# Scaling u out of PSUM, folding the row scale into q's decay factors, loading the skip diagonal, and a new order of table work and S5 in a two-layer hybrid trunk

## The chip, the core and the metric

One Trainium2 chip, one core. Times are microseconds of the core for one execution of the whole program; lower is better. The engines are TensorE (PE, with its weight loads PEld), VectorE (DVE), ScalarE (ACT), GpSimd (POOL) and SyncE (SP), which here issues the transfers. Each engine works through its own row of instructions in order and waits for others by semaphores.

## The reference, cut to what matters

Two layers on an input of 512 rows by 1024 features, all in float32. Each has a mixer and an FFN:

```
for i in range(DEPTH):                      # 2
    h = rmsnorm(x, norm_mix[i]);  z = h @ w_in[i]
    u, q, k, v, g, gate_lr = columns of z   # 512, 256, 256, 512, 512, 16
    y = s5(u)                               # 32 groups of 16 channels -> 64 complex states each
    y = gelu(y);  y = y * sigmoid(y @ w_glu + b_glu);  y_s5 = rmsnorm(y)
    y_gla = gla(q, k, v, g, gate_lr)        # 4 heads, chunks of 64 rows
    x = x + concat([y_s5, y_gla]) @ w_out[i]
    x = x + swiglu(rmsnorm(x))
return rmsnorm(x, norm_final)

# s5: s_t = a * s_(t-1) + bbar u_t;  y_t = Re(c s_t) + d_skip * u_t   (a, bbar, c complex)
# gla: log_a = log_sigmoid(gate_lr @ w_gate + b_gate) / 16;  cum = cumsum(log_a) in each chunk
#      q_dec = q / 8 * exp(cum);  k_inv = k * exp(-cum);  k_end = k * exp(last - cum)
```

## The kernel before

Tiles are 128 partitions by 512 rows of the sequence. Each float32 matrix product is made of three: weights and input are split into a high and a low part (whi, wlo; x0h, x0l and so on), and `mm3` adds whi·xh, whi·xl and wlo·xh (L576 to L578). A dense tile has eight blocks of 128 by 128, so 24 matmuls. The weights come as a stream of units of 1024 columns, eight blocks each: `Weights` loads a unit (raw, L142, SP's queue, two buffers), casts it on ScalarE (whi, L163) and takes the difference on VectorE (wlo, L165), three buffers of each. In layer 0's input projection unit 3 holds u(3), units 4 to 7 q and k of the two head pairs, units 8 to 10 three tiles of g, units 11 to 14 v; wlo3 below is the difference of unit 3.

The row scale rstd of the norm isn't applied to the input; the results are multiplied with it instead. It is made after the first two u tiles (`stats`), as rs_mix on ScalarE. With it VectorE makes rsb (L706), the input of the gate matmul gt (L768). u(b), one of four tiles, is copied by ScalarE in 16 pieces of 32 by 128 from PSUM into the layout U that S5 wants (L745), and then scaled there (L738) by rU, rstd laid out alike (L687). The gates run through `gate_a` (matmul, logistic), `gate_c` (cumulative sum by a scan, L783, L784, L786) and `gate_b` (three exponentials E, Ei, Ee for each head pair hp). `q_tile` multiplies q with E and then, in quarters of 64 by 256, with rstd, into two zeroed buffers qz:

```
nc.vector.scalar_tensor_tensor(e, ps, 0.125, e, op0=M, op1=M)          # L807
...
nc.gpsimd.memset(qz[i][r, :, 1 - d], 0.0)                                # L813
nc.vector.tensor_tensor(qz[i][r, :, d], e[..], R["rstd"][..], op=M)      # L814
```

S5 works in chunks of four rows, with the complex states of a block of channels turned by tables cosT and sinT, so that a real scan does the recurrence. For each of four blocks b: `s5_fwd` makes x (L833) from U and the table Wk, turns it with four products on VectorE (L841 to L844) and two sums on GpSimd (ro, L846, L847), and scans eight times (L852); `s5_back` turns back (L866, L867, L872, L873) with sr and sm on GpSimd (L869, L874); `s5_y` makes y from the tables Tz and Vx (L888, L890), and ScalarE takes the gelu in 16 pieces (L899); `y_split` casts the result for the GLU (yg, L583).

The tables themselves depend on the parameters and are made in the kernel: small vectors a1 to a4, fr, fi (`prep_small`, 128 by 32, L304 and neighbours), complex products (`cplx`, eight operations: four of 128 by 256, L407 to L410, and halves), transposes on VectorE (L441) and copies by DMA into Wk (`prep_w`, L446, four a transpose), Vx and Tz (`prep_v`, with the skip diagonal idd in four operations at L498), cosT and sinT (`prep_rot`: angles rf at L538 to L544, cosines on ScalarE, six operations L567 to L572 on GpSimd for each quarter). Layer 1's tables are made during layer 0's FFN. Layer 0's are made beside its input projection: four generators, moved on by calls of bg() between the tiles, `bg0` with the table BG_W saying which.

PE, ACT and SP issue in the order of the program text. DVE does so in the first part of layer 0's mixer (to `region.close()`) and in the FFN; elsewhere a scheduler orders DVE, and POOL throughout, by priorities and due operands.

## Time and profile before

| | before |
|---|---|
| median of 3 executions | 1160.08 us (1159.53 to 1160.54) |
| profiled execution | 1159.86 us, span 1158.1 us |
| TensorE busy | 1110.1 us (96% of the span), 5316 matmuls |
| VectorE busy | 706.2 us (61%) |
| ScalarE busy | 485.6 us (42%) |
| GpSimd busy | 331.9 us (29%) |

The span runs from the first to the last instruction of the profiled execution; its own time is 1.76 us longer. The shares are averages over the whole program: layer 0's mixer takes the first 170 us or so, its FFN and layer 1 follow, and in the two FFNs TensorE works nearly without a gap. What an engine costs in a stretch is read from that stretch.

### The profile page before, as it was taken

How to read it: one execution, taken by the hardware profiler on the slowest of the kernel's cores; microseconds unless marked ns; L12 is line 12 of the kernel's file. 1: busy time of each engine (PE TensorE's matmuls, PEld its weight loads, DVE VectorE, ACT ScalarE, POOL GpSimd, SP SyncE). 2: the span in 40 equal slices, each digit the busy share in tenths (PEclk: the TensorE clock that was granted, in tenths of full speed). 3: DMA queues.
4: the chain of work that ended last, by engine and by line, in shares of the span. 5: the costliest groups of instructions: out<-in, count | busy, mean ns of one | idle time of the engine just before them, and what ended most of it. 6: DMA issues, size and time to landing. Idle time of an engine off the chain costs nothing.

```text
span 1158.1 us, 13973 instructions
## 1 busy us (share of the span) xinstructions
PE 1110.1 (96%) x5316; PEld 913.9 (79%) x5316; DVE 706.2 (61%) x947; ACT 485.6 (42%) x844; POOL 331.9 (29%) x322
## 2 busy tenths in 40 slices
PE   8789779999999999999999799999999999999997
PEld 5568658888888888888887688888888888888886
DVE  7996976866454454564466994686545444444454
ACT  6853458443232232432358653745323222222243
POOL 6899544546000052065030440352000000000003
PEclk9899889999999999999999999999999999999999
DMA  6155111244343523232331212123332333223221
GB/s 211 55 112 126 37 37 37 92 130 116 103 109 100 137 91 101 82 109 91 93 104 41 73 61 85 56 91 94 107 100 85 106 99 102 91 91 109 91 91 73
DMA packets 64099, 107.72 MB, mean 93 GB/s; under 512 B 37408, under 2 KB 38304, under 8 KB 64032
## 3 DMA queue, kind: packets, MB, share of 16 engines
q1 hardware_dynamic: 63888, 106.56, 30.2%
q8 instruction: 42, 0.69, 0.2%
q10 hardware_dynamic: 144, 0.26, 0.1%
q14 instruction: 25, 0.20, 0.1%
HBM read 100.52 MB, written 2.10 MB: 89 GB/s over the span
## 4 chain that ended last, share of the span: by engine, by line
PE 79%; DVE 12%; ACT 3%; issue 2%; POOL 2%; DMA 1%; SPq 1%; DVEq 0%; POOLq 0%; ACTq 0%
PE fg L576 7%; PE fg L577 7%; PE fg L578 7%; PE fu L578 7%; PE fu L576 7%; PE fu L577 7%; PE fo L578 7%; PE fo L576 7%; PE fo L577 7%; DVE ro L852 2%; DVE wlo L165 2%; ACT U L745 1%; DVE qz L814 1%; DMA wrr<-in_wr_dram 1%; DMA raw<-in_wst_dram 1%
## 5 line engine op out<-in xcount | busy, mean ns | idle before, releaser
L165 DVE TENSOR_TENSOR wlo<-raw,whi 128x1024 fp32r<-128x1024 f32 x182 | 242.2, 1333 | 113.2 <-ACT whi L163 112.0
L163 ACT CAST whi<-raw 128x1024 fp32r<-128x1024 f32 x183 | 191.8, 1050 | 280.0 <-PE fo L577 116.9
L602 POOL TENSOR_TENSOR sq_fin<-sq_fin 128x512 f32<-128x512 f32 x5 | 6.5, 1296 | 341.8 <-ACT sq_fin L598 341.8
L1237 DVE TENSOR_TENSOR fu<-fu,rs_ffn 128x512 f32<-128x512 f32 x44 | 30.4, 691 | 116.7 <-PE fu L578 113.9
L1254 DVE TENSOR_TENSOR xall<-xall,fo 128x512 f32<-128x512 f32 x78 | 53.1, 686 | 61.9 <-PE fo L578 61.7
L1234 DVE TENSOR_TENSOR fg<-fg,rs_ffn 128x512 f32<-128x512 f32 x44 | 30.3, 688 | 34.7 <-PE fg L578 30.8
L1236 ACT ACTIVATE fg<-fg 128x512 f32<-128x512 f32 x44 | 27.7, 629 | 42.5 <-DVE fg L1234 42.4
L899 ACT ACTIVATE y<-y 32x128 f32<-32x128 f32 x128 | 34.4, 269 | 20.9 <-PE y L890 17.3
L1238 DVE TENSOR_TENSOR fu<-fg,fu 128x512 f32<-128x512 f32 x44 | 31.3, 711 | 5.7 <-ACT fg L1236 1.3
L745 ACT COPY U<-u 32x128 f32<-32x128 f32 x128 | 32.9, 257 | 1.5
L852 DVE TENSOR_TENSOR_SCAN ro<-sp_mag,ro 128x128 f32<-128x128 f32 x64 | 28.5, 507 | 6.6 <-POOL ro L846 6.6
L1089 POOL TENSOR_TENSOR xall<-xall,wo 128x512 f32<-128x512 f32 x16 | 25.5, 1613 | 24.0 <-DVE wo L1088 24.0
L407 POOL TENSOR_TENSOR pt<-bc,sp_a1r 128x256 f32<-128x256 f32 x2 | 1.7, 852 | 94.0 <-issue 92.0
L568 POOL TENSOR_TENSOR rt<-rg 128x512 f32<-128x512 f32 x8 | 10.2, 1288 | 59.8 <-ACT rg L548 59.7
L602 POOL TENSOR_TENSOR sq_s<-sq_s,sq_s 128x512 f32<-128x512 f32 x6 | 8.1, 1342 | 64.3 <-ACT sq_s L598 64.3
L869 POOL TENSOR_TENSOR sr<-ro,ro 128x508 f32<-128x508 f32 x8 | 14.6, 1826 | 39.3 <-DVE ro L867 39.3
L602 POOL TENSOR_TENSOR sq_x1nmix<-sq_x1nmix 128x512 f32<-128x512 f32 x7 | 9.2, 1315 | 57.3 <-ACT sq_x1nmix L598 57.3
L890 PE MATMUL y<-sr,Vx 128*128 128x128 f32 x64 | 15.0, 322 | 8.0 <-POOL sr L869 7.8
L890 PE MATMUL y<-sm,Vx 128*128 128x128 f32 x64 | 14.8, 318 | 6.2 <-POOL sm L874 6.2
L888 PE MATMUL y<-U,Tz 128*128 128x128 f32 x64 | 14.9, 320 | 5.5 <-DVE ro L842 5.4
L846 POOL TENSOR_TENSOR ro<-ro,ro 128x512 f32<-128x512 f32 x8 | 10.7, 1344 | 30.8 <-DVE ro L843 30.8
L890 PEld LDWEIGHTS y<-sr,Vx 128*128 128x128 f32 x64 | 11.9, 231 | 8.9 <-POOL sr L869 8.9
(1257 smaller groups left out, 3533.0 us busy)
## 6 DMA issues: line engine op xcount, KB each, us to landing
raw<-in_wst_dram SPq DMA_DIRECT2D x183, 512.0 KB, 3.5
Wk<-wt SPq DMA_DIRECT2D x64, 64.0 KB, 3.9
xall<-in_xt_dram SPq DMA_DIRECT2D x3, 512.0 KB, 8.5
out_dram<-fin SPq DMA_DIRECT2D x6, 256.0 KB, 2.2
bc<-in_s5bc_dram SPq DMA_DIRECT2D x4, 256.0 KB, 4.1
raw<-in_wst_dram SPq DMA_DIRECT2D x1, 384.0 KB, 5.8
cst<-in_const_dram SPq DMA_DIRECT2D x1, 384.0 KB, 5.0
xall<-in_xt_dram SPq DMA_DIRECT2D x1, 283.0 KB, 3.0
```

What stands on the lines that cost most here:

```text
L163: self.nc.scalar.copy(hi, raw)
L165: (self.nc.gpsimd if v in POOL_W else self.nc.vector).tensor_tensor(lo, raw, hi.bitcast(F32), op=ALU.subtract)
L576: nc.tensor.matmul(ps, whi, xh, start=start, stop=False)
L577: nc.tensor.matmul(ps, whi, xl, start=False, stop=False)
L578: nc.tensor.matmul(ps, wlo, xh, start=False, stop=stop)
L745: nc.scalar.copy(u[32 * t:32 * t + 32, j].rearrange("p (n c) -> p n c", n=NCH), pv[32 * j:32 * j + 32, :, t, :],)
L852: v.tensor_tensor_scan(dst[:, cs], sp["mag4"][:, c:c + 1].to_broadcast([P, P]), src[:, cs], 0.0, M, A)
L890: nc.tensor.matmul(o, Vx[:, pr, part, 1:].rearrange("p a b c -> p (a b c)"), s_[:, cs], start=False, stop=(part == 1),)
L899: nc.scalar.activation(yv[32 * j:32 * j + 32, :, t, :], ps[32 * t:32 * t + 32, j * P:(j + 1) * P].rearrange("p (n c) -> p n c", n=NCH), AF ...
L1237: nc.vector.tensor_tensor(u, pu, rstd[0], op=M)
L1238: nc.vector.tensor_tensor(u, g, u, op=M)
L1254: nc.vector.tensor_tensor(xT[n], xT[n], ps[n], op=A)
```

## The change

- u is scaled straight out of PSUM: one product of the tile with rstd into us on VectorE, and ScalarE's 16 copies read us instead of PSUM. rU goes. In layer 0 the copies come later: those of u(1) in `u_tile(3)`, of u(2) behind q(0), of u(3) behind k(0).
- E is multiplied with rstd as a whole (`gate_d`), and qz is written from PSUM with E in four operations. The qz buffers are allotted once and zeroed at the start.
- The skip diagonal is laid out on the host and loaded (64 KB a layer); the four operations of L498 go.
- The product with a4 for layer 0's Vx goes from GpSimd to VectorE.
- A table TABLES takes BG_W's place: at each call, a letter for each step of a generator (s small, w Wk, v Vx, r rotations).
- The scans become a function of their own, `s5_scan`; GpSimd's S5 operations get high priority; x(0) stands ahead of v, and the other S5 steps are spread anew over v's eight parts.

```diff
-    NACT = 45
+    NACT = 41
...
+    qz = [[cp.tile([P, 4, 2, 64], F32, name=f"qz{hp}{i}") for i in range(2)] for hp in range(2)]
...
+        idd = act(f"idd{l}")[:, 0:P]
+        nc.sync.dma_start(idd, s5bc[l][:, 4 * 256:])
...
         for n in (1, 2, 3, 4):
-            cplx(e, l, cr, nci, spv(f"a{n}r", l), spv(f"a{n}i", l),
+            cplx(e[n - 1], l, cr, nci, spv(f"a{n}r", l), spv(f"a{n}i", l),
                  halves(Vx[:, :, 0, n]), halves(Vx[:, :, 1, n]), conj=True)
             yield
-        idd = act(f"idd{l}")
-        for b in range(NB):
-            r = slice(32 * b, 32 * b + 32)
-            nc.vector.tensor_tensor(
-                idd[r, 0:P].rearrange("p (a b) -> p a b", a=4),
-                bcast(C("ident")[r, 32 * b:32 * b + 32], [32, 4, 32], 1),
-                bcast(S(l, "dskip")[r, 4 * b:4 * b + 4], [32, 4, 32], 2), op=M,
-            )
-        yield
...
-                unit_rows()
+                for b in range(2):
+                    u_scale(b, ps[b])
                 if l == 0:
                     bg()
-                u_evac(0, ps[0])
+                else:
+                    u_copy(0)
...
             gate_a(0)
             gate_a(1)
-            u_copy(1, ps[1])
+            u_scale(2, ps2)
+            if l == 0:
+                bg()
+            else:
+                u_copy(1)
             gate_c(0)
             gate_c(1)
-            u_scale(1)
-            u_evac(2, ps2)
+            if l == 0:
+                bg()
+                u_copy(0)
+            else:
+                u_copy(2)
...
+        def u_scale(b, ps):
+            t = us[b] = act(f"us{l}{b}")
+            nc.vector.tensor_tensor(t, ps, R["rstd"], op=M)
...
+        def gate_d(hp):
+            e = E[hp][0]
             d = dec[hp] = cp.tile([P, NCH], F32, tag=f"dec{hp}", name=f"dec{l}{hp}")
             nc.vector.tensor_copy(d, e.rearrange("p (n s) -> p n s", n=NCH)[:, :, 63])
-            E[hp] = (e, ei, ee)
+            nc.vector.tensor_tensor(e, e, R["rstd"], op=M)
...
-            nc.vector.scalar_tensor_tensor(e, ps, 0.125, e, op0=M, op1=M)
...
-                    nc.gpsimd.memset(qz[i][r, :, 1 - d], 0.0)
-                    nc.vector.tensor_tensor(
-                        qz[i][r, :, d], e[r, hf].rearrange("p (n t) -> p n t", n=4),
-                        R["rstd"][r, hf].rearrange("p (n t) -> p n t", n=4), op=M,
+                    nc.vector.scalar_tensor_tensor(
+                        qz[hp][i][r, :, d], ps[r, hf].rearrange("p (n t) -> p n t", n=4), 0.125,
+                        e[r, hf].rearrange("p (n t) -> p n t", n=4), op0=M, op1=M,
                     )
...
             q_tile(0)
+            u_copy(2)
             bg()
             k_tile(0)
+            u_copy(3)
             bg()
...
+            s5_fwd(0)
             bg()
+            s5_scan(0)
             region.close()
...
             v_tiles({
-                0: [bg, bg],
-                1: [lambda: s5_fwd(0), bg],
-                2: [lambda: s5_back(0), bg],
-                3: [lambda: s5_fwd(1)],
-                4: [lambda: score(0), lambda: s5_back(1), bg],
-                5: [lambda: s5_y(0), lambda: s5_fwd(2), bg],
-                6: [lambda: s5_y(1), lambda: s5_back(2), lambda: s5_fwd(3)],
-                7: [lambda: score(1), lambda: s5_back(3)],
+                0: [lambda: s5_back(0), bg],
+                1: [lambda: s5(1), bg],
+                2: [lambda: score(0), bg],
+                3: [lambda: s5_back(1), bg],
+                4: [lambda: s5_y(0), lambda: s5(2), bg],
+                5: [lambda: score(1), lambda: s5_back(2), bg],
+                6: [lambda: s5_y(1), lambda: s5(3)],
+                7: [lambda: s5_back(3)],
             })
+            y_split(0)
             s5_y(2)
-            y_split(0)
             y_split(1)
+            g_tile(3)
             y_split(2)
-            g_tile(3)
             s5_y(3)
...
-        BG_W = (1, 0, 2, 1, 1, 1, 1, 1, 1, 1)
+        TABLES = (
+            "s", "sv", "wr", "w", "ww", "wr", "wwr", "wwr", "wwv", "v", "r", "v", "r", "v", "", "v", "v",
+        )
```

How the rows of instructions change is shown at three places. A row has its line, the operation, out and in, and the shape; x4 means four alike. Line numbers differ between the two kernels.

VectorE in layer 0 around rsb, before (sptmp and sp_ names are small table vectors, rf and rk angles of the rotations, rs_mix the row scale):

```order
L544 TENSOR_TENSOR rf_243<-rf_243,rk_244 128x384
L304 TENSOR_TENSOR sptmp<-lam 128x32 x2
L304 TENSOR_TENSOR sptmp<-sptmp 128x32
L165 TENSOR_TENSOR wlo_306<-raw_199,whi_305 128x1024
L352 RECIPROCAL sptmp<-sptmp 128x32
L706 TENSOR_TENSOR rsb_342<-r_333,rs_mix_358 128x512
L687 COPY rU_370<-rs_mix_358 32x128 x4
```

and of the change:

```order
L305 TENSOR_TENSOR sp_a1i<-sptmp 128x32
L305 TENSOR_TENSOR sp_a1r<-sptmp 128x32
L165 TENSOR_TENSOR wlo_291<-raw_207,whi_290 128x1024
L694 TENSOR_TENSOR rsb_327<-r_318,rs_mix_343 128x512
L732 TENSOR_TENSOR us_355<-u_262,rs_mix_343 128x512
L732 TENSOR_TENSOR us_357<-u_263,rs_mix_343 128x512
L344 TENSOR_SCALAR sptmp<-sp_a1r 128x32
```

rsb and the first two us now stand directly behind wlo3; the angles of the rotations and thirteen small operations that stood ahead come later.

SP's queue in layer 0, from the third group of Wk copies on, before (wt is a transposed table, raw a unit of weights):

```order
L446 DMA Wk<-wt_689 32x16x32 x4
L142 DMA raw_769<-in_wst_dram 128x1024
L446 DMA Wk<-wt_738 32x16x32 x4
L142 DMA raw_824<-in_wst_dram 128x1024
L446 DMA Wk<-wt_790 32x16x32 x4
L142 DMA raw_870<-in_wst_dram 128x1024
L446 DMA Wk<-wt_836 32x16x32 x4
L142 DMA raw_910<-in_wst_dram 128x1024
L446 DMA Wk<-wt_883 32x16x32 x4
L142 DMA raw_957<-in_wst_dram 128x1024
L446 DMA Wk<-wt_930 32x16x32 x4
L142 DMA raw_1025<-in_wst_dram 128x1024
```

and of the change:

```order
L450 DMA Wk<-wt_713 32x16x32 x4
L450 DMA Wk<-wt_761 32x16x32 x4
L142 DMA raw_801<-in_wst_dram 128x1024
L450 DMA Wk<-wt_767 32x16x32 x4
L450 DMA Wk<-wt_813 32x16x32 x4
L142 DMA raw_853<-in_wst_dram 128x1024
L450 DMA Wk<-wt_819 32x16x32 x4
L450 DMA Wk<-wt_866 32x16x32 x4
L142 DMA raw_907<-in_wst_dram 128x1024
L142 DMA raw_958<-in_wst_dram 128x1024
```

Copies and loads alternated; now raw_801 (unit 11), raw_853 (12) and raw_907 (13) each stand behind two groups of copies, and the last four groups close up.

TensorE where the g tiles end and v begins, before (kT is a transpose of Ee, v four tiles at once):

```order
L578 MATMUL g_932<-x7h,wlo_827 128x512
L935 MATMUL kT_966<-cst,Ee_593 128x128 x4
L913 MATMUL v_978<-whi_872,x0h 128x512
L914 MATMUL v_978<-wlo_873,x0h 128x512
```

and of the change:

```order
L573 MATMUL g_933<-x7h,wlo_804 128x512
L936 MATMUL kT_967<-cst,Ee_533 128x128 x4
L827 MATMUL x_974<-U_475,Wk 128x128 x4
L827 MATMUL x_975<-U_475,Wk 128x128 x4
L914 MATMUL v_1010<-whi_855,x0h 128x512
```

x(0) stood behind the first two of v's eight parts (24 matmuls) and now stands ahead of them all.

## Rows read from the trace of the kernel before

**Rows 1.** Page, busy tenths of TensorE in 40 equal slices.

```profile
PE   8789779999999999999999799999999999999997
```

**Rows 2.** Waits of TensorE: line waited for: us in total, times, longest.

```profile
PE y L890 <- POOL sr L869: 7.8, 4, 3.3
...
PE gt L768 <- DVE rsb L706: 5.2, 1, 5.2
```

**Rows 3.** Timelines of ScalarE and VectorE at the gates: start, us, engine, line, operation.

```profile
29.81 0.63 ACT L614 ACTIVATE rs_mix<-rs_mix 128x512 f32<-128x512 f32 x1
...
30.74 4.27 ACT L745 COPY U<-u 32x128 f32<-32x128 f32 x16
...
34.66 1.21 DVE L165 TENSOR_TENSOR wlo<-raw,whi 128x1024 fp32r<-128x1024 f32 x1
...
36.06 0.62 DVE L706 TENSOR_TENSOR rsb<-r,rs_mix 128x512 f32<-128x512 f32 x1
```

**Rows 4.** Window: us, busy PE, PEld, DVE, ACT, POOL, TensorE's clock, DMA share, GB/s.

```profile
20.00:62.00 42.00, 32.52 (x134) 22.43 (x133) 41.06 (x82) 37.44 (x88) 32.71 (x35) 0.92 0.16 51
```

**Rows 5.** VectorE's groups, 20 to 160 us: busy us, mean ns | idle before.

```profile
L498 DVE TENSOR_TENSOR idd<-cst,xall 32x128 f32<-32x128 f32 x4 | 3.9, 973 | 0.1
L738 DVE TENSOR_TENSOR U<-U,rU 128x512 f32<-128x512 f32 x4 | 3.7, 955 | 0.0
...
L784 DVE TENSOR_TENSOR_SCAN ab<-cst,mn 128x512 f32<-128x512 f32 x2 | 3.1, 1528 | 0.1
```

**Rows 6.** Line L814 in layer 0: ns min/median/max, first and last start.

```profile
L814 DVE TENSOR_TENSOR qz<-E,rs_mix x8: 416/870/1193, 71.7 to 83.0; 64x256 f32<-64x256 f32 x8
```

**Rows 7.** Timelines of TensorE and VectorE around q(1), with the idle time before.

```profile
62.38 0.79 PE L578 MATMUL q<-x0h,wlo 128*128 128x512 f32 x1 [2.93 <-DVE wlo L165]
...
63.57 0.42 DVE L407 TENSOR_TENSOR pt<-bb,sp_a1r 128x256 f32<-128x256 f32 x1
...
68.06 1.16 DVE L417 TENSOR_TENSOR wk<-pt 64x256 f32<-64x256 f32 x2
```

**Rows 8.** DMA issues, 0 to 130 us: count, KB each, median us to landing.

```profile
raw<-in_wst_dram SPq DMA_DIRECT2D x17, 512.0 KB, 4.1
Wk<-wt SPq DMA_DIRECT2D x32, 64.0 KB, 3.5
xall<-in_xt_dram SPq DMA_DIRECT2D x3, 512.0 KB, 8.5
```

**Rows 9.** Timelines of SP's queue and TensorE at x(0).

```profile
96.01 2.71 SPq L446 DMA_DIRECT2D Wk<-wt  x4
...
101.47 1.13 PE L833 MATMUL x<-U,Wk 128*128 128x128 f32 x8 [1.00 <-DMA Wk<-wt]
```

**Rows 10.** GpSimd's groups, 26 to 160 us, and its timeline at S5(0)'s sum.

```profile
L415 POOL TENSOR_TENSOR Vx<-pt 64x256 f32<-64x256 f32 x8 | 7.0, 875 | 0.5
L569 POOL TENSOR_TENSOR cosT<-cosT,rt 128x512 f32<-128x512 f32 x4 | 6.1, 1540 | 0.0
...
L567 POOL TENSOR_TENSOR cosT<-rk 128x512 f32<-128x512 f32 x4 | 4.4, 1120 | 0.1
...
112.49 1.29 POOL L846 TENSOR_TENSOR ro<-ro,ro 128x512 f32<-128x512 f32 x1
```

**Rows 11.** VectorE's timeline: the first scans and the end of S5 in layer 0.

```profile
113.81 4.54 DVE L852 TENSOR_TENSOR_SCAN ro<-sp_mag,ro 128x128 f32<-128x128 f32 x4 [4.61 <-POOL ro L846]
...
156.25 0.69 DVE L873 TENSOR_TENSOR rp<-ro,cosT 128x512 f32<-128x512 f32 x1
```

**Rows 12.** Timelines of ScalarE and TensorE ahead of the GLU's last quarter.

```profile
164.39 0.63 ACT L1001 ACTIVATE th<-g 128x512 f32<-128x512 f32 x1 [2.81 <-DVE g L992]
...
170.22 0.50 PE L576 MATMUL gl<-yg03h,whi 128*128 128x512 f32 x1 [3.04 <-ACT yg03h L583]
```

**Rows 13.** Layer 1: timelines of VectorE at the gates and TensorE at y(1).

```profile
624.92 1.18 DVE L784 TENSOR_TENSOR_SCAN ab<-cst,mn 128x512 f32<-128x512 f32 x1
...
660.91 0.49 PE L890 MATMUL y<-sr,Vx 128*128 128x128 f32 x2 [3.32 <-POOL sr L869]
```

115 lines of the change are left out of this document (54 added, 61 removed).

## The prediction, made before the changed kernel was run

> **What bounds the kernel now.** I read the page's slices first, then the waits of TensorE, then the timeline of each engine around those waits, from late to early. The slices are 28.95 us each, and TensorE is 90% busy or more in all but seven [rows 1]: the first three, the fifth and sixth (116 to 174 us), one in layer 1 (637 to 666), the last. In the FFN TensorE works without a gap, so what layer 0's mixer wins or loses ahead of it shifts the end by as much. The waits of TensorE name the places [rows 2]: 5.2 us at the gate matmul for rsb on VectorE, 7.8 us at S5's outputs for sr on GpSimd.
>
> At the gates, ScalarE has rstd ready at 29.81 + 0.63 = 30.44, but VectorE starts rsb only at 36.06, behind table operations and the weight difference of 34.66 [rows 3]. This isn't an idle VectorE that looks away: from 20 to 62 us it is busy for 41.06 of 42.00 us [rows 4]. So the order can be bettered there and the amount of work stays the limit.
>
> The second place is S5. VectorE stands idle for 4.61 us until GpSimd's sum ro (started at 112.49, behind rotation tables) lets the first scans start at 113.81 [rows 10, 11]. From there VectorE works nearly without a break through the four blocks of S5, to 156.25 + 0.69 = 156.94 [rows 11]. Then the last block's y must be read out, put through gelu and cast before the GLU's last quarter starts at 170.22, 3.04 us late [rows 12]. This chain ends last in layer 0's mixer; what moves the first scans moves the end.
>
> **The change part by part.** The profiled execution took 1159.86 us (span 1158.10); the median of three is 1160.08, 0.22 above. All sums are in that execution's microseconds.
>
> *Gates first.* In the new order rsb and the two us stand behind one weight difference (1.2, as at 34.66), with the 13 small table operations behind them. rsb can start at about 30.9, so the 5.15 us wait goes. But VectorE has to do nearly all the same work before the next weight difference that TensorE waits for, wlo6 (TensorE resumed there at 62.38, [rows 7]). Before, from 34.66 to the end of that difference it is 27.7 us. Added are 3.3 of small operations that stood ahead and 4.4 for the seven rotation-angle operations. Taken off are 0.9 (copies rU), 0.7 (first transpose), 1.2 (three U scales at 0.955 become three from PSUM at rsb's 0.62, which reads PSUM too: [rows 3, 5]) and 2.0: the gates' operations now run while GpSimd has little to do, and the scan L784 takes 1.53 beside GpSimd here and 1.18 in layer 1 [rows 5, 13]; the same for the two others of each pair. That is 30.6 from a start at 29.2: wlo6 is done at 59.8, against 62.34, **-2.5 us**. TensorE reaches that point near 50 now and waits for some ten us there: the wait has moved.
>
> *q and the tables behind it.* Before, one product and four of E by rstd, 0.42 us each at their fastest and 0.87 in the median, all in SBUF [rows 6]. Now one product of E by rstd, ahead of the end of q, and four straight from PSUM. The trace has none of that form: between 0.42 and 0.87 each; I take 0.43, since they read one operand from SBUF, where the slow ones of the old form read two beside GpSimd. That makes 1.0 + 4 x 0.43 for each head pair, 1 us less than the 3.7 before. Next come the eight table operations that took 5.65 us from 63.57 to 69.22 [rows 7], taken unchanged. By this TensorE resumes the first g tile at about 74.2.
>
> *S5 ahead of v.* Before, x(0) stood behind the first two parts of v, and waited for the last Wk copies for only 1.0 us: they were issued from 96.01 to 98.72, and TensorE went on at 101.47 [rows 9]. Now x(0) stands directly behind the g tiles and kT, which TensorE reaches at 74.2 + 5.0 + 5.45 + 5.45 + 0.7 = 90.9. Wk's last copies can't be there: their transposes stand behind weight differences on VectorE, whose raw loads stand behind earlier Wk copies in SP's queue. Following the loop: transposes 3 and 4 done at 85.0; raw11 issued at 83.2, lands 4.1 later at 87.3; its difference done at 89.6; the sixth transpose at 90.9; two groups of Wk copies of 1.3 each, issued 92.3 to 94.9; landing 3.5 later, 98.4 [rows 8]. So **a new wait of about 7 us at x(0)**, which is done at 99.4. It is hidden as long as S5(0) starts earlier than before, since TensorE has the whole of v to do while S5(0) is on VectorE, and some 5 us of slack at the later y.
>
> *a4 and the skip diagonal.* The four skip operations (3.9 us, [rows 5]) stood right ahead of S5(0) on VectorE; a load of 64 KB takes their place, long before. In their stead VectorE gets the eight operations of a4, 5.65 us by the eight of [rows 7] that it ran beside GpSimd. Behind wlo12 they run from 96.9 to 102.6, then wlo13, g and S5(0)'s four products: done at 106.5. A rule of the Trainium skill speaks against that move: by "SBUF — State Buffer", section "Who interferes with whom", a VectorE instruction with two SBUF operands and a GpSimd instruction that reads SBUF lock each other out completely. On that rule the eight would take about 13 us, which is a rival below.
>
> *GpSimd.* It loses a4's eight operations and the zeroing of qz. Its rotations wait for ScalarE's cosines. In the new order these stand behind three sets of sixteen U copies (4.27 us a set, [rows 3]), from 54.7 on by my count, and casts, bk copies, a table load and the cosines themselves are 7.4 more: 74.9. Until S5(0)'s sum there are 18 rotation operations (six groups of 1.12 to 1.54, in the mean 1.37) and a3's eight at 0.875, as L415 [rows 10]: 74.9 + 24.7 + 7.0 = 106.6. So both operands meet there: the sum starts at 106.6 and the scans at 107.9, against 112.49 and 113.81, **-5.9 us**.
>
> *To the end of layer 0's mixer.* Four scans took 4.54 us beside rotations at 113.81; with the tables further on, S5(0) saves 0.7 more, and the run of VectorE through the other blocks 0.2: it ends at 150.1, against 156.94, -6.8. The last sm follows, y(3) ends at 156.6. Before, the sixteen gelu of y(3) also stood behind th on ScalarE, whose input came late (164.39 + 0.63, and the GLU 5.2 us behind that, [rows 12]); y(3) then no longer meets it, so the GLU's last quarter goes on at about 162.0: **-8.2 us**.
>
> *Layer 1.* TensorE's order is the same. VectorE saves a U scale, but the copies start 1.0 later, since the scaling stands ahead of them, and qz(1)'s four operations (3.5 us before, four of the median in [rows 6]) now stand ahead of the scans of S5(1) in part. y(1) waits 3.32 us for sr now, and goes on at 660.91 [rows 13]; I get 662.8: **+1.9 us**. Between nothing, if the order evens out, and 3.5, if all four are in the way, that is about the middle.
>
> *Sum.* -8.2 + 1.9 = -6.3: 1153.6. As the sum of S5(0) waits for the later of two chains that I have within 0.1 us of each other, I add 0.4: 1154.0; the 0.22 to the median is within that.
>
> **Rivals.** *GpSimd still holds S5(0).* If its rotations cost 1.54 each, as the dearest group [rows 10], that is 3.1 more, and a3 at 1.02 in place of 0.875 an operation 1.2 more: the sum starts at 110.9, the gain shrinks by 4.3 to 2.0, **1157.9**. For it: GpSimd has had less rest than any in this stretch. Against: beside TensorE's wait VectorE reads PSUM more often.
>
> *a4 locked.* If each of the eight waits out a whole rotation operation, 8 x (0.27 + 1.37) = 13.1 in place of 5.65: S5(0)'s products are done 7.4 later, at 114.0, and all of the gain is gone, **1160.9**. Against it: in [rows 7] the eight took 5.65 us beside GpSimd operations of like kind.
>
> *Slower: the loop of loads and Wk copies.* Each weight load in SP's queue has Wk copies ahead of it and decides when the next transpose comes. If raw11 and raw12 take 8.5 us each, as the first loads of the program do [rows 8], x(0) is done 8.8 later, at 108.2, the sum starts at 115.4, and the result is +2.5; with raw13 late as well +6.9: **1162.4 to 1166.8**. It decides from the point where the sum starts later than 112.9. Against: loads in the first 130 us have a median of 4.1.
>
> *More.* If the loop and GpSimd are each 2.5 us better than I have them (operations at 1.27, qz without disturbance) and layer 1 stays as it is, -6.3 - 2.5 - 1.9: **1149.2**.
>
> **How the numbers follow.** The forecast has 0.52, with 1150 to 1157.5 as its own range (the wait at x(0) by two us either way, layer 1 from 0 to 3.5); GpSimd 0.16, a4 0.06, the loop 0.11, more 0.15. A measurement of this kernel tells about 0.2% (2.3 us) from no change: under 1157.8 is faster, over 1162.4 slower. Faster: 0.50 + 0.15 + 0.05 of GpSimd's = 0.70. Same: 0.02 + 0.11 + 0.04 = 0.17. Slower: 0.11 + 0.02 = 0.13. The range 1146.5 to 1161.5 leaves out the loop (0.11) and about 0.05 below.
>
> **What the changed profile would show.** If I am right: no wait at gt; a wait of 8 to 12 us for wlo in front of q(1); 6 to 8 us at x(0) for Wk; the first scans at 107 to 109; the last rp of layer 0 at about 149.5 and the GLU's last quarter at about 162; in layer 1 the wait of y(1) for sr above 4. I am wrong if the wait at x(0) exceeds 12 us, if a4's operations on VectorE take over 1 us each, or if GpSimd's sum stays at 111 or later. If S5(0) comes early and the GLU doesn't, TensorE's own work (v behind x) is the limit instead.

## The result, and the profile after

The change makes the kernel slower: 1166.27 us in the median of four executions (1164.30 to 1167.95) against 1159.80 for the kernel before beside it, a ratio of 1.0055 [1.0037, 1.0073]. The profiled execution took 1165.76 us, span 1164.0 against 1158.1. Of these 5.9 us, 3.1 are lost in layer 0's mixer and 2.8 behind it: the first GLU tile reaches its last quarter at 173.47 in place of 170.22, the second at 179.49 in place of 176.37, and from there to the end of the span it is 984.5 us, 981.7 before.

The waits of TensorE, longest first, with the line waited for, us in total, times, longest:

```profile
PE q L573 <- DVE wlo L165: 11.5, 1, 11.5
PE x L827 <- DVE g L993: 7.9, 1, 7.9
PE y L891 <- POOL sr L869: 7.5, 4, 4.7
PE sc L974 <- DVE ro L836: 6.9, 1, 6.9
```

The 5.2 us for rsb of [rows 2] are gone, and three waits of 6.9 to 11.5 us have come in layer 0. VectorE's timeline at the gates, and TensorE's at q(1):

```profile
29.00 1.60 DVE L165 TENSOR_TENSOR wlo<-raw,whi 128x1024 fp32r<-128x1024 f32 x1 [1.92 <-ACT whi L163]
30.53 0.68 DVE L694 TENSOR_TENSOR rsb<-r,rs_mix 128x512 f32<-128x512 f32 x1
...
61.54 0.79 PE L573 MATMUL q<-x0h,wlo 128*128 128x512 f32 x1 [11.48 <-DVE wlo L165]
```

rsb starts 5.5 us earlier than in [rows 3], and TensorE resumes q(1) 0.84 earlier than in [rows 7]. SP's queue from the third group of Wk copies on; a row of x8 spans two groups of four:

```profile
76.00 10.94 SPq L450 DMA_DIRECT2D Wk<-wt  x8
87.04 0.56 SPq L142 DMA_DIRECT2D raw<-in_wst_dram  x1
87.70 5.46 SPq L450 DMA_DIRECT2D Wk<-wt  x8
93.26 0.56 SPq L142 DMA_DIRECT2D raw<-in_wst_dram  x1
```

The first row isn't eight copies back to back: its second group, the fourth in all, waits for its transpose on VectorE.

```profile
83.60 0.71 DVE L445 STREAM_TRANSPOSE wt<-wk 128x512 f32<-128x512 f32 x1
...
84.34 2.60 SPq L450 DMA_DIRECT2D Wk<-wt  x4
```

Eight copies in a row take 5.46 us to issue, 2.7 for a group, as the row of four in [rows 9] does. So raw11 is issued at 87.04, 3.8 later than forecast, and raw12 at 93.26. x(0)'s wait is named for g, whose scaling on VectorE stood behind the difference of unit 12; in e9 below the wait at the same place, 7.36 us to 100.49, is named for Wk. Both come out of this queue. VectorE from the difference of unit 12 to the first scans, and GpSimd's sum between:

```profile
98.90 1.28 DVE L165 TENSOR_TENSOR wlo<-raw,whi 128x1024 fp32r<-128x1024 f32 x1 [3.25 <-ACT whi L163]
...
100.70 0.67 DVE L411 TENSOR_TENSOR pt<-bc,sp_a4r 128x256 f32<-128x256 f32 x1
...
106.07 0.85 DVE L419 TENSOR_TENSOR Vx<-pt 64x256 f32<-64x256 f32 x2
...
110.49 0.68 DVE L838 TENSOR_TENSOR ro<-x,cosT 128x512 f32<-128x512 f32 x1
...
110.65 1.28 POOL L841 TENSOR_TENSOR ro<-ro,ro 128x512 f32<-128x512 f32 x1 [1.34 <-DVE ro L837]
...
111.97 4.29 DVE L851 TENSOR_TENSOR_SCAN ro<-sp_mag,ro 128x128 f32<-128x128 f32 x4 [0.80 <-POOL ro L841]
```

The eight operations of a4 take 6.2 us, not far from the 5.65 forecast, but start 3.8 us late; the sum now waits for VectorE, and the scans start 1.8 us earlier than in [rows 11], not 5.9. VectorE in the other blocks (first product of blocks 1 and 2; the scans of block 1; the last rp), and GpSimd beside the scans of block 1:

```profile
120.59 0.69 DVE L835 TENSOR_TENSOR ro<-x,cosT 128x512 f32<-128x512 f32 x1
...
128.42 4.30 DVE L851 TENSOR_TENSOR_SCAN ro<-sp_mag,ro 128x128 f32<-128x128 f32 x4 [1.02 <-POOL ro L841]
...
130.83 1.30 POOL L567 TENSOR_TENSOR sinT<-sinT,rt 128x512 f32<-128x512 f32 x1
...
133.36 1.36 DVE L851 TENSOR_TENSOR_SCAN ro<-sp_mag,ro 128x128 f32<-128x128 f32 x4
...
137.68 0.69 DVE L835 TENSOR_TENSOR ro<-x,cosT 128x512 f32<-128x512 f32 x1
...
161.92 0.68 DVE L873 TENSOR_TENSOR rp<-ro,cosT 128x512 f32<-128x512 f32 x1
```

From the first scans to the end of the last rp it is 50.6 us (111.97 to 162.60), 43.1 before [rows 11]. Block 1 alone takes 17.1 us (12.6 before). GpSimd still makes rotation tables beside it, the last until 132.1. Then y(3) comes late and TensorE goes on as in [rows 12], 3.25 us later:

```profile
166.82 0.63 ACT L1002 ACTIVATE th<-g 128x512 f32<-128x512 f32 x1 [1.92 <-DVE g L993]
...
168.23 4.48 ACT L900 ACTIVATE y<-y 32x128 f32<-32x128 f32 x16 [0.27 <-PE y L891]
...
173.47 0.50 PE L571 MATMUL gl<-yg03h,whi 128*128 128x512 f32 x1 [1.96 <-ACT yg03h L578]
```

Layer 1: TensorE at y(0) and y(1); VectorE around qz(1); and windows, two of after and two of before, whose last three columns are the granted clock, DMA share and GB/s:

```profile
652.63 0.79 PE L891 MATMUL y<-sr,Vx 128*128 128x128 f32 x2 [4.65 <-POOL sr L869]
...
667.47 0.49 PE L891 MATMUL y<-sr,Vx 128*128 128x128 f32 x2 [1.36 <-POOL sr L869]
...
658.40 1.72 DVE L808 SCALAR_TENSOR_TENSOR qz<-q,E 64x256 f32<-64x256 f32 x4
660.13 2.64 DVE L851 TENSOR_TENSOR_SCAN ro<-sp_mag,ro 128x128 f32<-128x128 f32 x8
...
652.00:656.00 4.00, 2.93 (x12) 2.64 (x13) 4.00 (x7) 2.04 (x3) 4.00 (x4) 0.50 0.01 2
668.00:672.00 4.00, 3.31 (x16) 3.31 (x17) 4.00 (x5) 0.87 (x1) 3.18 (x5) 0.61 0.01 2
...
660.00:664.00 4.00, 2.17 (x11) 1.98 (x12) 3.96 (x5) 1.87 (x5) 2.26 (x2) 0.83 0.10 42
664.00:668.00 4.00, 4.00 (x30) 4.00 (x29) 4.00 (x6) 1.46 (x6) 2.59 (x4) 0.75 0.00 0
```

The long wait is at y(0), and y(1) waits less than in [rows 13]. TensorE's clock is at its lower level (0.50, 1.2 of 2.4 GHz) after y(0)'s wait, and falls again at 668. Before, it fell once in this stretch, behind y(1) (the last two rows).

### The profile page after: what moved, and what is told of

The parts are those of the page before. It is cut to its first block, busy times and chain, and to the rows that moved or that the text cites. A ratio compares the mean times of both kernels' runs of the same rounds, so it can differ in the third digit from the quotient of the medians.

```text
span 1164.0 us, 13947 instructions
## 1 busy us (share of the span) xinstructions
PE 1110.4 (95%) x5316; PEld 916.3 (79%) x5316; DVE 704.7 (61%) x939; ACT 490.3 (42%) x844; POOL 312.1 (27%) x302
## 4 chain that ended last, share of the span: by engine, by line
PE 80%; DVE 8%; ACT 5%; POOL 3%; issue 1%; SPq 1%; DMA 1%; DVEq 0%; POOLq 0%; ACTq 0%
PE fg L572 7%; PE fg L571 7%; PE fu L571 7%; PE fg L573 7%; PE fu L572 7%; PE fu L573 7%; PE fo L573 7%; PE fo L572 7%; PE fo L571 7%; DVE ro L851 2%; ACT U L739 2%; DVE wlo L165 1%; PE y L891 1%; SPq L450 1%; DMA wrr<-in_wr_dram 1%
## 5 line engine op out<-in xcount | busy, mean ns | idle before, releaser
L165 DVE TENSOR_TENSOR wlo<-raw,whi 128x1024 fp32r<-128x1024 f32 x182 | 246.8, 1359 | 129.0 <-ACT whi L163 127.7
L739 ACT COPY U<-us 32x128 f32<-32x128 f32 x128 | 37.8, 295 | 2.9 <-DVE us L732 1.0
L562 POOL TENSOR_TENSOR cosT<-rk 128x512 f32<-128x512 f32 x8 | 11.8, 1480 | 61.5 <-ACT rk L544 61.5
L827 PE MATMUL x<-U,Wk 128*128 128x128 f32 x128 | 17.8, 297 | 7.9 <-DVE g L993 7.9
L827 PEld LDWEIGHTS x<-U,Wk 128*128 128x128 f32 x128 | 17.1, 212 | 8.6 <-DVE g L993 8.2
```

The source lines that it names most:

```text
L165: (self.nc.gpsimd if v in POOL_W else self.nc.vector).tensor_tensor(lo, raw, hi.bitcast(F32), op=ALU.subtract)
L739: nc.scalar.copy(u[32 * t:32 * t + 32, j].rearrange("p (n c) -> p n c", n=NCH), pv[32 * j:32 * j + 32, :, t, :],)
L827: nc.tensor.matmul(ps[part][:, j * P:(j + 1) * P], Wk[:, part, 4 * b + j], U[b][:, j], start=True, stop=True,)
```

## The experiments

Each run is timed against the kernel before on the same chip. *Scans* is where the first scans of layer 0 start, *S5 end* the end of its last rp, *GLU* the start of the first tile's last quarter, *rest* the span from the same point of the second GLU tile on; all from the profiled executions, in us.

| kernel | median | ratio [95%] | scans | S5 end | GLU | rest |
|---|---|---|---|---|---|---|
| before | 1159.80 | 1 | 113.81 | 156.94 | 170.22 | 981.7 |
| after | 1166.27 | 1.0055 [1.0037, 1.0073] | 111.97 | 162.60 | 173.47 | 984.5 |
| e1_u_layer1_old | 1166.81 | 1.0059 [1.0044, 1.0074] | 111.89 | 162.47 | 173.31 | 984.2 |
| e2_a4_gpsimd | 1168.55 | 1.0075 [1.0058, 1.0091] | 113.15 | 164.72 | 177.08 | 984.8 |
| e3_cosines_first | 1172.07 | 1.0105 [1.0090, 1.0120] | 118.80 | 168.28 | 179.20 | 984.5 |
| e4_third_raw | 1177.56 | 1.0154 [1.0138, 1.0169] | 118.26 | 169.71 | 183.69 | 985.7 |
| e5_defer_wk | 1162.74 | 1.0025 [1.0014, 1.0035] | 108.47 | 158.81 | 170.76 | 984.7 |
| e6_score_late | 1167.39 | 1.0065 [1.0050, 1.0080] | 112.00 | 162.51 | 175.02 | 984.5 |
| e7_q_layer1_old | 1163.25 | 1.0035 [1.0021, 1.0050] | 111.82 | 162.44 | 173.30 | 982.0 |
| e8_before_skip_q | 1163.72 | 1.0036 [1.0023, 1.0049] | 118.15 | 158.31 | 171.60 | 983.9 |
| e9_defer_q1old | 1160.10 | 1.0005 [0.9995, 1.0014] | 109.17 | 159.47 | 170.32 | 982.2 |
| e10_defer_v_first | 1160.83 | 1.0007 [0.9998, 1.0016] | 117.27 | 157.21 | 170.46 | 982.2 |
| e11_defer_cosines | 1161.96 | 1.0018 [1.0008, 1.0027] | 111.33 | 160.59 | 171.44 | 982.4 |
| e12_before_q_own_buffers | 1161.56 | 1.0015 [1.0006, 1.0024] | 112.58 | 155.67 | 168.96 | 984.6 |
| e13_half_rotations | 1153.76 | 0.9948 [0.9932, 0.9965] | 106.40 | 152.78 | 163.63 | 982.1 |
| e14_before_half_rotations | 1152.32 | 0.9937 [0.9920, 0.9953] | 106.13 | 149.03 | 162.31 | 981.7 |
| e15_layer1_e_gpsimd | 1162.77 | 1.0026 [1.0016, 1.0036] | 108.60 | 158.93 | 169.77 | 984.7 |
| e16_before_best | 1156.07 | 0.9970 [0.9958, 0.9982] | 112.55 | 155.63 | 166.26 | 981.6 |

**First round: one piece at a time, in the changed kernel.** e1 gives layer 1 the old order of u back (copies from PSUM, scaling by rU behind them):

```diff
+                    unit_rows()
                     u_copy(0)
+                    u_mul(0)
...
         def u_scale(b, ps):
+            if l:
+                us[b] = ps
+                return
```

> Undone in layer 1 alone: u is copied from PSUM and scaled afterwards, as in the kernel before; layer 0 and q stay changed. In the changed kernel layer 1 loses about 2.6 us (the end of layer 0's mixer 3.25 late, the end of the program 5.9 late). Theory (ScalarE's copies wait for us, its cast of the next weights comes later, S5(0) with it): the loss goes, 1163.2 to 1163.8 against 1165.8 profiled, and y(0) of layer 1 waits about 2.3 us for sr again, not 4.65. Rival (q's two operations ahead of S5's scans cost it): no change, and y(0) still waits over 4.

The rest stays at 984.2 (y(0) waits 2.85, but y(1) 3.63, and the clock falls twice as well): u's order alone isn't what costs layer 1. e2 takes a4 back to GpSimd:

```diff
-prep_v(0, 3 * [nc.gpsimd] + [nc.vector], pl)
+prep_v(0, 4 * [nc.gpsimd], pl)
```

> a4's eight operations of layer 0 go back to GpSimd, all else is the change. Theory (both engines' table work meets at S5(0)'s sum): VectorE is 6.2 us earlier at S5(0)'s products (done near 105 in place of 111.2), GpSimd about 6 later, so the sum starts near 113 to 116 against 110.65, and the time is 1167 to 1170. Rival (VectorE alone holds S5(0), since GpSimd waited 1.34 us for it): the sum starts near 105 to 107 and the time falls to about 1161.

The scans come 1.2 later and the GLU 3.6, and the time is 2.3 us longer in the median, though the two intervals overlap: a4 on VectorE seems worth having. VectorE's products were done at 110.1, only 1.1 earlier than after: it waited 4.79 us for the next unit of weights instead. So something ahead of a4 is late too. e3 puts the cosines ahead of u's copies on ScalarE, to let GpSimd start early:

```diff
+            if l == 0:
+                next(rots)
             u_copy(b if l else 1)
```

> ScalarE makes the cosines of layer 0's rotations right behind the gates' exponentials, ahead of three sets of u's copies, so GpSimd needn't wait 7.5 us for them. Theory A (GpSimd's late rotations lengthen S5's blocks: in block 1 four scans take 4.30 beside them, the difference 2.24, and the sum comes 1.0 late): the rotations end 6 to 8 us earlier, the stretch from block 1's first product to block 2's shrinks from 17.1 to 12.5 to 14 us, and the time falls by 3 to 4.5, to about 1162. Theory B (the loop of loads and Wk copies holds all of it): first scans stay at 112, blocks keep their lengths, the time stays within 1 us of 1166.

Neither theory was met, and the run says nothing on GpSimd's start: the first table transpose waited 5.27 us for ScalarE, the whole loop of transposes, copies and loads moved by 6 to 7, and so did the scans. e4 has a third buffer for the loads, to take them out from behind the copies, and two work tiles fewer to make room (NACT counts them: the pool of 128 by 512 buffers that both the tables and the tiles in work are taken from):

```diff
-    NACT = 41
+    NACT = 39
...
-            self.load(v + 1)
+            self.load(v + (2 if v >= 6 else 1))
```

> A third buffer for raw weights, so that from unit 8 on each load stands one pair of Wk copies earlier in SP's queue. Theory B (the loop: raw12 is issued at 93.26 behind five Wk groups of 2.7 us each, its difference waits 3.25 for the cast, and a4 and S5(0) come behind it): that wait goes, S5(0)'s products end about 3 us earlier, the first scans at 109 to 110 against 112.0, the time falls by 1.5 to 3. Theory A (GpSimd's tables hold S5): the first scans gain at most the 1.3 us that GpSimd's sum waited, the blocks stay long, the time falls by less than 1.

It says nothing on the buffer: with two tiles fewer the first transpose waited 5.23 us for GpSimd and wlo7 came 4.3 us late (67.46 for 63.12).

**Second round: the loop, the masks, q.** e5 holds each Wk copy back until the next call of bg0, so that the loads go first; the text of the kernel moves nothing else:

```diff
         def place(part, d, tr):
+            if l == 0:
+                held_wk.append((part, d, tr))
+            else:
+                issue(part, d, tr)
...
+            while held_wk:
+                issue_wk[0](*held_wk.pop(0))
             for c in
```

> Only SP's order changes in layer 0: each group of Wk copies is issued one step of the table work later, so that a weight load no longer stands behind copies whose transpose is only just issued. Theory (a loop holds S5(0): raw11 waits in SP's queue for the fourth transpose, which VectorE does behind q(1), and a4 and S5(0)'s products stand behind the differences of raw12 and raw13): raw11 is issued by about 80 in place of 87.0, the waits of 2.84 and 3.25 us for whi go, S5(0)'s products end 3 to 5 us earlier than 111.2, and the time falls by 1.5 to 4 us, to 1162 to 1165. Rival (GpSimd holds it; its sum waited only 1.34 us for VectorE): the first scans move by no more than 1.3 us and the time by less than 1.

SP's queue in e5:

```profile
73.59 5.64 SPq L142 DMA_DIRECT2D raw<-in_wst_dram  x2
79.28 7.21 SPq L458 DMA_DIRECT2D Wk<-wt  x8
86.67 0.48 SPq L142 DMA_DIRECT2D raw<-in_wst_dram  x1
```

raw11 is the second load of the first row: it goes before 79.28 and no longer at 87.04, and raw12 at 86.67, not 93.26. The difference of unit 12 starts at 92.78 in place of 98.90, the scans at 108.47 (forecast for the change: 107.9), and the kernel gains 3.5 us. So the loop cost S5(0) its start. How its price divides between the copies' issue time and the transposes they wait for, e5 doesn't tell: it takes both out of the loads' way. e6 moves score(1) with its masks from v's part 5 to part 7:

```diff
-                5: [lambda: score(1), lambda: s5_back(2), bg],
+                5: [lambda: s5_back(2), bg],
...
-                7: [lambda: s5_back(3)],
+                7: [lambda: score(1), lambda: s5_back(3)],
```

> score(1) goes back behind v's eighth part, where the kernel before had it. Theory (TensorE stands at score(1) for 6.9 us, until VectorE has read x(2), and its mask copies fall into S5's block 2, which grew from 9.7 to 14.0 us, in place of filling block 3's wait for GpSimd): block 2 shrinks by 1.8, TensorE's wait goes, layer 0's mixer ends 1 to 2 us earlier: 1164 to 1165. Rival (VectorE does the same sum of work either way and is the limit): within 0.7 us of 1166.3.

Block 2 shrinks from 14.0 to 11.2 us and block 3 grows by as much (a wait of 3.06 for the sum); S5 ends where it did, and the GLU starts 1.6 later. e7 takes q's fold out of layer 1 alone:

```diff
+            if l:
+                nc.vector.scalar_tensor_tensor(e, ps, 0.125, e, op0=M, op1=M)
...
+                    if l:
+                        nc.vector.tensor_tensor(qz.., e.., R["rstd"].., op=M)
+                        continue
```

> q undone in layer 1 alone (product with E from PSUM, then four products with rstd in SBUF, into the same fixed buffers); u and layer 0 stay changed. With u undone alone, S5's products of layer 1 came as early as before but for 0.7 us of E by rstd ahead of them, and y(0) still waited 2.85 us and then ran at half TensorE's clock. Theory (E by rstd on VectorE ahead of S5(0)'s turn, and u's copies, make y(0)'s wait long enough that the clock falls; either alone does it): y(0) still waits over 3 us, the granted clock still falls to about 0.5 there, and layer 1 loses 1.5 to 2.5 us still: 1165 to 1166.5. Rival (q alone is the cause): y(0) waits 2.3, no fall at y(0), layer 1 loses nothing: 1163 to 1164.

TensorE at y(0), y(1) in layer 1 of e7, VectorE around q(1), and a window:

```profile
651.83 0.80 PE L900 MATMUL y<-sr,Vx 128*128 128x128 f32 x2 [4.05 <-POOL sr L878]
...
666.04 0.49 PE L900 MATMUL y<-sr,Vx 128*128 128x128 f32 x2 [0.48 <-POOL sr L878]
...
657.50 0.68 DVE L806 SCALAR_TENSOR_TENSOR E<-q,E 128x512 f32<-128x512 f32 x1
658.10 2.62 DVE L860 TENSOR_TENSOR_SCAN ro<-sp_mag,ro 128x128 f32<-128x128 f32 x8
660.64 1.69 DVE L812 TENSOR_TENSOR qz<-E,rs_mix 64x256 f32<-64x256 f32 x4
...
668.00:672.00 4.00, 4.00 (x35) 3.92 (x35) 4.00 (x7) 2.12 (x8) 2.74 (x4) 1.00 0.39 131
```

The rest is 982.0, as before but for 0.3. y(0) waits nearly as long as after, with its stretch at the lower clock; what is gone is the second fall, behind y(1), which waits 0.48 in place of 1.36. In the old form one product of 0.68 us frees PSUM and the four qz go behind the scans; in the folded form all four read PSUM and stand ahead (1.72 us, then the scans at 660.13).

e8 goes the other way: the kernel before, with the loaded skip diagonal and q folded in both layers, qz in fixed buffers and 41 work tiles as in the change.

```diff
-    NACT = 45
+    NACT = 41
...
+    qz = [[cp.tile([P, 4, 2, 64], F32, name=f"qz{hp}{i}") for i in range(2)] for hp in range(2)]
```

> The kernel before with two parts of the change alone: the skip diagonal loaded, and E by rstd folded with fixed qz buffers, in both layers; u, the table order, a4 on GpSimd and S5's place as before. Theory (these two take work off: 3.9 us of VectorE and 2.4 us of GpSimd's zeroing ahead of S5(0)'s sum, which then starts at about 110 in place of 112.5; layer 1 may lose up to 2.4 by the clock at y(0)): the mixer of layer 0 ends 2 to 2.5 us earlier, the time is 1157.5 to 1160. So the loss of the whole change lies in its new order. Rival (q's fold costs in layer 0 too): 1161 or more.

The old order with these parts can't spare four work tiles: the second transpose waited 5.17 us for Wk copies to release one, and the sum came at 116.83.

**Third round: does an earlier S5(0) end layer 0 earlier?** e9 joins e5 and e7.

> Both edits that brought something, together: Wk copies issued a step later, q undone in layer 1. If the two losses are apart (the loop in layer 0's input projection; the second fall of TensorE's clock in layer 1), the gains add: 3.5 + 3.0 from 1166.3, so 1159.5 to 1160.5, about the time of the kernel before, with S5(0)'s first scans still 5 us earlier than there. If they are one, only 1162.5.

The two gains add up, to the time before and no further, though the scans start 4.6 us earlier. e10 is e9 with the steps of S5 put back where they were, x(0) behind the first two parts of v:

```diff
-            s5_fwd(0)
             bg()
-            s5_scan(0)
...
-                0: [lambda: s5_back(0), bg],
-                1: [lambda: s5(1), bg],
...
+                0: [bg, bg],
+                1: [lambda: s5(0), bg],
+                2: [lambda: s5_back(0), bg],
...
```

> As the last, and x(0) back behind two of v's eight parts, with S5's other steps where the kernel before had them. Theory (TensorE waits 7.5 us at x(0) for Wk, then works it off at half clock, 3.75 us in place of 1.95; with v in that gap neither happens, and S5(0)'s products begin at most 1 us later or up to 1.8 earlier): 0.5 to 2 us faster than the last. Rival (S5 ahead of v is what gives the earlier scans): S5(0)'s products begin 3 us or more later, and the time is 1.5 us or more slower.

The first scans and the last rp on VectorE, of e9:

```profile
109.17 5.34 DVE L869 TENSOR_TENSOR_SCAN ro<-sp_mag,ro 128x128 f32<-128x128 f32 x4 [0.80 <-POOL ro L859]
...
158.79 0.68 DVE L891 TENSOR_TENSOR rp<-ro,cosT 128x512 f32<-128x512 f32 x1
```

and of e10:

```profile
117.27 2.43 DVE L869 TENSOR_TENSOR_SCAN ro<-sp_mag,ro 128x128 f32<-128x128 f32 x4 [3.06 <-POOL ro L859]
...
156.53 0.68 DVE L891 TENSOR_TENSOR rp<-ro,cosT 128x512 f32<-128x512 f32 x1
```

With scans that start 8.1 us later, e10's S5 ends 2.3 earlier. That it isn't faster by these 2.3 comes from ScalarE: the gelu of y(3) stands behind th there, as in [rows 12], and starts at 165.29, in e9 at 165.09. Both expectations missed: the products begin 4 us later than in e9 (109.95 for 105.91), and the time is the same within the noise. Either way, the early scans brought S5's end no nearer, and that is the end of the forecast's central step.

e11 is e9 with u's last two copies on ScalarE behind k(1) and g(0), so that cosines and rotations come some 8 us earlier.

```diff
             q_tile(0)
-            u_copy(2)
             bg()
             k_tile(0)
-            u_copy(3)
             bg()
...
+            u_copy(2)
```

> As the first of these, with ScalarE's cosines of layer 0 behind q(0) (behind the bk copies this time, so the loop isn't delayed) and the copies of u(2) and u(3) behind k(1) and g(0). Theory (GpSimd waits 7.5 us for the cosines; its rotations run into S5's blocks 0 and 1, where four scans take 5.3 and eight 4.6 us beside them in place of 1.4 and 2.7): rotations start at 68 to 69, end by 120; blocks 0 and 1 shrink by 3 to 5 us together, and the time falls by 2 to 4 us, to 1156 to 1158. Rival (whi of the next units now comes behind the cosines and the loop is late again, as when they stood ahead of all copies): x(0) later than 101, no gain.

The forecast gain didn't come. Rotations start at 69.5, but then GpSimd waits 3.99 and 2.02 us for transposes that now come later, and wlo12 waits 5.94 for its cast.

e12 is e8 with qz taken from the pool and zeroed each time, so that all 45 tiles stay:

```diff
-    NACT = 41
+    NACT = 45
...
+            qz = [act(f"qz{l}{hp}{i}", F32, (P, 4, 2, 64)) for i in range(2)]
...
+                    nc.gpsimd.memset(qz[i][r, :, 1 - d], 0.0)
```

> The kernel before with the skip diagonal loaded and E by rstd folded, but qz from the pool of work tiles, zeroed each time, and the pool at 45 tiles, as before. With fixed buffers and 41 tiles the second transpose waited 5.17 us for a Wk copy to free its tile and S5(0)'s sum came at 116.8, 4.3 later than in the kernel before. Theory (four tiles fewer hold the table work up): that wait is gone, the sum starts at 110 to 112.5, layer 0's mixer ends 0 to 2.5 us earlier than in the kernel before; with layer 1's loss of about 2.4 the time is 1159.5 to 1162. Rival (the fold itself holds it): the sum still starts after 115, 1163 or more.

Now skip and fold are worth something in layer 0 (S5 ends 1.3 earlier, the GLU starts 1.3 earlier), and the folded q costs layer 1 its 2.9 here too, in the old order.

**Fourth round: what holds S5's end.** e13 and e14 leave twelve of the 24 rotation operations of layer 0 out (the tables of blocks 2 and 3 are not made), in e9 and in the kernel before:

```diff
+            if l == 0 and b in (2, 3):
+                yield
+                continue
             e.tensor_tensor(co, coarse(k)
```

> Work left out: as the version with deferred Wk copies and q of layer 1 undone, but layer 0's rotation tables of blocks 2 and 3 aren't made (12 of 24 GpSimd operations, some 16 us), so the output isn't the reference's. There S5(0)'s first scans start at 109.2, 4.6 us earlier than in the kernel before, and the mixer of layer 0 ends no earlier. Theory (the rotation work left behind S5(0)'s sum sits in blocks 0 and 1 and slows the scans beside it): S5's last product on VectorE comes 4 to 6 us earlier than 159.5, the time falls by 3 to 5 us. Rival (the sum of VectorE's own work, weight differences and masks that moved into the blocks, is the limit): less than 2 us.

> Work left out: the same 12 operations in the kernel before. Theory (there GpSimd's rotations hold S5(0)'s sum at 112.5, behind VectorE's products at 108.2): the sum starts at 108 to 109, S5 ends 4 us earlier or more, the time falls by 2.5 to 4 us. Then rotation work costs about the same ahead of the sum as behind it, and an earlier S5(0) can't win by itself. Rival: less than 1.5 us.

VectorE's last rp in e13 (e9's is above):

```profile
152.10 0.68 DVE L894 TENSOR_TENSOR rp<-ro,cosT 128x512 f32<-128x512 f32 x1
```

S5 ends 6.7 us earlier than in e9 and, in e14, 7.9 earlier than before. In the old order all of it comes at the first scans (7.7 earlier); in the new one only 2.8 there and 3.9 in blocks 0 and 1 (first scans to block 2's first product: 25.3 us in e9, 21.4 in e13). The rotation work costs nearly the same whether it stands ahead of the scans or beside them, and more than either expectation had.

e15 is e5 with layer 1's u as before and its product of E by rstd on GpSimd.

```diff
-            nc.vector.tensor_tensor(e, e, R["rstd"], op=M)
+            (nc.gpsimd if l else nc.vector).tensor_tensor(e, e, R["rstd"], op=M)
```

> Deferred Wk copies; in layer 1 u as in the kernel before, q folded as in the change, but E by rstd on GpSimd, which has nothing to do there. With u undone and E by rstd on VectorE, y(0) waited 2.85 us and y(1) 3.63, and TensorE's clock fell at both. Theory (0.7 us of E by rstd ahead of S5's turn decides at y(0)): y(0) waits about 2.2 us, without a fall of the clock there; one fall at most in layer 1; the time is 1158 to 1160.5. Rival (q's four products ahead of the scans of S5(1) cost it): both falls stay, 1161.5 to 1163.

The loss stays, 984.7: y(0) waits only 2.69 and keeps the full clock, and y(1) waits 4.67, 1.3 more than in [rows 13], and the clock falls there to 0.50. So the loss can come as one longer wait, with a single fall, and its time fits the rival's range though only one of the rival's two falls is there. That leaves the four products that read q from PSUM.

e16 puts together what helped, on the kernel before: loaded skip diagonal, q folded in layer 0 only with qz from the pool, and th of the last g tile behind the gelu of y(3) on ScalarE:

```diff
-            nc.scalar.activation(t, g, AF.Tanh, scale=0.5)
...
             late.append(lambda: y_split(3))
+            late.append(th_held.pop())
```

> The kernel before with what helped or cost nothing: skip diagonal loaded, E by rstd folded in layer 0 alone with qz from the pool, u, table order and S5's place as before, and th of the last g tile behind the gelu of y(3) on ScalarE. Theory: S5 ends about 3 us earlier in layer 0 (as with the fold in both layers), yg03h no longer waits for th (4.62 us there), layer 1 loses nothing: the GLU's last quarter goes on near 164.5 to 166 against 170.2, and the time is 1154 to 1156.5. Rival (something else is late there, the first three quarters or the clock): 1158 or more.

ScalarE and TensorE ahead of the GLU's last quarter in e16:

```profile
161.10 4.46 ACT L904 ACTIVATE y<-y 32x128 f32<-32x128 f32 x16 [0.83 <-PE y L895]
...
166.12 0.62 ACT L1008 ACTIVATE th<-g 128x512 f32<-128x512 f32 x1
...
166.26 0.51 PE L570 MATMUL gl<-yg03h,whi 128*128 128x512 f32 x1 [1.96 <-ACT yg03h L577]
```

In e12 the gelu of the same y(3) started at 163.78, behind th, and the GLU at 168.96. e16 is 0.3% faster than the kernel before, and so the fastest of all that compute the whole result. Its profiled execution is the fastest of its six, 1.8 us below their median, so the rows above show it at its best.

## Why the prediction was wrong

**Right.** The wait at gt went, a wait of 11.5 us came at q(1) (forecast 8 to 12), a4's eight operations took 6.2 us (5.65), qz 1.73 for each tile (4 x 0.43), the rotations started at 77.2 (74.9). The wait of 7.9 at x(0) (6 to 8) has the size forecast by chance: TensorE got there at 92.90, not 90.9, and x(0) was done at 104.62, not 99.4. None of the three signs of being wrong that the prediction named came (the wait at x(0) was under 12, a4's operations took 0.78 each, the sum started at 110.65), so they were the wrong signs. Nor is TensorE's own work the limit, as its last sentence has it: TensorE waited 6.87 us at score(1) and 1.96 ahead of the GLU's last quarter.

**Gates: -2.5 forecast, -0.84 measured** at q(1). The stretch of VectorE to the end of wlo6 took 32.5 us, not 30.6: the seven operations on the angles took 5.6 (taken as 4.4), and the four weight differences 5.6 (4.7 before). (The 1.2 taken off for the U scales is 1.0 by the 0.955 and 0.62 that stand beside it.)

**"Two groups of Wk copies of 1.3 each."** This is the step that made S5(0) late. A group of four takes 2.6 to 2.7 us to issue; [rows 9] shows it, and the prediction itself has one group at 96.01 to 98.72. Of the 3.8 us by which raw11 is late, 1.3 are the price of the group ahead of it. The other 2.5 are its transpose: the copies could start only at 84.34, where the forecast's 83.2 less 1.3 leaves 81.9, on a VectorE that had been 1.7 late since wlo6 (done at 61.49, not 59.8). Each unit behind raw11 is late in turn: two groups more stand ahead of raw12, wlo12 starts at 98.90, the products of S5(0) are done at 111.2, not 106.5, and the scans start at 111.97, not 107.9. e5 shows the size: with the loads ahead of the copies, the scans start at 108.47. The slower rival had the right loop, and the wrong cause in it (long loads; the median to landing was 4.3 us). The measured time lies in its range, but by chance: it was to decide if the sum came later than 112.9, and the sum came at 110.65, and 2.8 of the loss are layer 1's.

**"What moves the first scans moves the end."** This is the step on which the whole gain stood, and it is wrong for this change. VectorE's scans and weight differences from the first scans to the last rp, two rows of before and two of after, with the idle time ahead of them:

```profile
L852 DVE TENSOR_TENSOR_SCAN ro<-sp_mag,ro 128x128 f32<-128x128 f32 x32 | 16.7, 583 | 6.6 <-POOL ro L846 6.6
...
L165 DVE TENSOR_TENSOR wlo<-raw,whi 128x1024 fp32r<-128x1024 f32 x2 | 2.4, 1214 | 0.0
...
L851 DVE TENSOR_TENSOR_SCAN ro<-sp_mag,ro 128x128 f32<-128x128 f32 x32 | 18.9, 649 | 5.7 <-POOL ro L841 5.7
L165 DVE TENSOR_TENSOR wlo<-raw,whi 128x1024 fp32r<-128x1024 f32 x3 | 4.6, 1547 | 0.0
```

Of the idle time, 4.61 us before and 0.80 after lie ahead of the first scans. So of the 7.5 us by which the stretch grew, 2.2 are longer scans, 2.9 longer waits for GpSimd's sums, and 2.2 weight differences: one more stands inside, and another took 2.24 us beside GpSimd, not 1.2. (The masks of score take 3.5 us in both.)

Behind this stands the order of GpSimd's work. Before, its rotations were over at 117.75, and 22 of the 24 stood ahead of S5(0)'s sum:

```profile
116.34 1.41 POOL L572 TENSOR_TENSOR sinT<-sinT,rt 128x512 f32<-128x512 f32 x1
```

In the change the sums of S5 go first, and six operations come behind the first sum, until 132.1, four of them beside scans. The forecast's own count says so, 18 ahead of the sum; yet it took off 0.7 us "with the tables further on". Four scans take 1.36 us when GpSimd is idle and 4.3 to 5.3 beside it: each of the four lasts about as long as one operation of GpSimd. The eight of a4 ran beside shorter ones, mostly halves of Vx (1.77 and 1.66 us for two), and so took 0.78 each. The rule of the Trainium skill that the prediction weighed for a4 ("SBUF — State Buffer", section "Who interferes with whom": a VectorE instruction with two SBUF operands and a GpSimd one that reads SBUF lock each other out) agrees with both rows; it should have been asked of the scans, and for a4 with the operations that stood beside it.

e10 starts scans 8 us later than e9 and loses nothing, e6 moves the masks and gains nothing, e13 and e14 take out GpSimd's work and gain 6.3 us (to e9) and 7.2 us (to the kernel before) in the median. In the old order an earlier start does move the end, as e14 shows, where work is taken out ahead of it; the change moved the work behind the start instead. So the limit of that stretch is the work of VectorE and GpSimd together, not the start of one chain. The prediction had the sentence on VectorE (busy 41 of 42 us, "the amount of work stays the limit") for the gates, and didn't ask it of S5.

The -8.2 at the GLU was to come from the same step plus 1.4 from th getting out of gelu's way. Measured is +3.25. The idea on th was sound: e16 does just that.

**Layer 1: +1.9 forecast, +2.8 measured,** right in sign and near in size. The forecast named two causes. u's copies alone aren't one (e1: 984.2). The four qz ahead of S5(1)'s scans are: without them (e7) the rest is 982.0, with them in the kernel before (e12) 984.6, and without them there (e16) 981.6. The way is not the one forecast: y(1)'s wait was to grow and fell to 1.36, y(0)'s grew to 4.65, and TensorE's four waits for y in layer 1 take 7.2 us in all, 7.3 before. What was added is one stretch more of TensorE at the lower clock, two in place of one.

**Not forecast: work tiles.** Fixed qz buffers take four from the pool. In the old order this costs 2.2 us (e8 against e12, 1163.72 and 1161.56, the zeroing of each tile included). What it costs within the changed order wasn't run; e4, with two more taken, suggests that it is tight there too. The sum of terms is then: loop 3.5 (e5), layer 1 2.5 to 3.0 (e7, 1166.27 to 1163.25), and nothing gained by the order of S5 (e9 against e10, 1160.10 and 1160.83).

**Open.** That S5(0)'s early start gains nothing is shown by e9, e10 and e13 for this amount of GpSimd work and 41 work tiles. How the loss divides between scans, waits for GpSimd and weight differences was read from rows, not run apart. That 45 tiles would have let the new order gain something stands untested.

## What to carry to other kernels

Before a chain's start is credited to its end, add up what each engine has yet to do until that end: where the sum of work fills the stretch, an earlier start only changes where the rest of the work falls, and an experiment that takes work out tells it at once. A load in a queue starts behind all that stands ahead of it: count the issue time of each group from a row of that group, and when the last of them has what it copies. A product that reads PSUM in four pieces makes all four urgent, where one product that copies and four from SBUF let the four wait.
